# Order of the raw weight loads of a seven-product group: the sum s3 third, the quarter a12 fourth

## The chip, the cores and the metric

The kernel runs on one core of a Trainium2 chip. The metric is the device time of one execution in microseconds. The kernel before takes 1626.28 us, the median of three runs that lie between 1625.93 and 1626.74 us. All times below are microseconds unless ns is written; a time such as "at 1041.06" counts from the first instruction of the profiled execution.

The engines are named as the profile names them: PE does the matrix products (PEld is its weight load, which lies beside them), DVE is the vector engine, ACT the scalar engine, POOL the GpSimd engine, SP the engine that only issues transfers. Each engine works through its own instructions in order.

## The reference

The reference is a decoder trunk of two layers on 512 tokens of width 1024, all in 32-bit floats. Its shape, cut to what matters here:

```python
for l in range(DEPTH):                                   # 2 layers
    x = x + 0.5 * swiglu(rms_norm(x, ...), ffn1_wg[l], ffn1_wu[l], ffn1_wd[l])
    h = rms_norm(x, mix_norm[l])
    z = h @ w_in[l]                                      # attention and short convolution
    x = x + concat([attn_out, conv_out]) @ w_out[l]
    x = x + 0.5 * swiglu(rms_norm(x, ...), ffn2_wg[l], ffn2_wu[l], ffn2_wd[l])
return rms_norm(x, final_norm)

def swiglu(h, w_gate, w_up, w_down):
    return (jax.nn.silu(h @ w_gate) * (h @ w_up)) @ w_down
```

The gate and up weights are 1024 x 2816, the down weights 2816 x 1024, so nearly all the work is the product of 512 tokens with large weight matrices that are each used once. Every weight comes from memory as 32-bit floats.

## The kernel before

**Two words per number.** PE multiplies numbers of a shorter format, so each weight tile is split into two words: ACT casts the raw tile to `wh`, DVE subtracts that from the raw tile and gives the rest, `wl` (both on line 228, function `split`). The activations are split in the same way. A product is then three matrix products: `wh` with the high word, `wh` with the low word, `wl` with the high word.

**Seven products instead of eight.** Most of the weights go through a scheme of the Strassen-Winograd kind. A group takes a matrix of weights as four quarters a11, a12 (first index 0: the gate weights, or the left half of the outputs of a down projection) and a21, a22 (the up weights, or the right half), and multiplies seven forms of them, in this order (`FORMS`, line 38): a11, a12, s2, s3, s1, a22, s4. Signs aside, s1 is a21 with a22 added, s2 is a11 with s1 added, s3 is a21 with a11 added (the gate sum's unit), and s4 is a12 with s2 added. Each form has two halves of 128 x 1024 elements, so a group is 14 half products, and each half product in a feed-forward block is 12 matrix instructions on PE. In the chain of work a whole product (two halves, 24 instructions) is one line.

**Raw units.** The function `seven` (line 375) lists what is loaded for a group, as ten units of 512 KB, two halves each: before the change a11, s1, a12, s3, a22. The units of s1 and s3 have two sources. The first is loaded by SP as all units are (line 210); the second is added on the way by an accumulating transfer that POOL issues (line 223). s2 is made in place of a11 by an addition on DVE (line 269), and s4 in place of a12 (line 291 on DVE; line 289, an accumulating transfer from POOL, in the groups whose `how` is `"share"`).

**What sets the order.** `need_split` (line 236) walks through the list of all forms of the kernel. For each it first calls `need_raw` (line 212), which issues loads up to a given unit, then emits the cast and the subtraction. `take_split` calls it two half products ahead of PE (`SPLIT_AHEAD = 2`). How far the loads run ahead is set by the table `last` and `LOAD_AHEAD = 4`: at form `what`, half `h`, units up to `u + max(last, 4) + h + 4` are asked for, where `u` is the group's first unit. The loads go to SP in the order of the units, whatever the order of their use. They land in a pool of 8 buffers (tag `raw`, line 123), so a load waits until an earlier unit has been used for the last time. The split words have three buffers each (tags `wh` and `wl`, lines 272 and 273): the cast of half product n waits until PE has finished half product n-3.

The order of the instructions on each engine is fixed when the program is built: a scheduler takes them by the order in which they are written and by its own estimate of when each can start. Some orders are forced with `tc.issue_after`. One matters here: in the groups of the down projections, whose s2 is of the kind `"share"`, the DVE addition that makes the first half of s2 comes after the subtraction emitted last, which is that of the second half of a12 (`state["rest"]`, lines 264 to 269).

**Stages.** Each feed-forward block runs a plain stage (`p`), a narrow down projection (`d`), five gate-and-up groups (`w`, at 1, 3, 5, 7, 9), two groups of the down projection (`s`, at 1 and 5) and a last narrow one (`d`); the last block of the kernel ends instead with a group of its own (`e`), whose load and form order stand in `END_LOADS` and `END_FORMS`, apart from those of the other groups. The mixer's `w_out` is one more group. That makes 29 groups that `seven` builds: per layer 10 gate-and-up groups and one of `w_out`, and in all 7 of down projections. In this text the group ("s", 1) of a block is called the *first down group*, ("s", 5) the *second down group*; there are four of the first and three of the second. In a gate-and-up group ACT and DVE also gate the results; in the down groups they add results to the residual, and in the first down group they split the last forms of the activations as well.

Of the kernel before, what the change touches and what calls it, by code (L numbers as in the profile page):

```python
# [75 lines left out]
def trunk_kernel(  # L76
# [118 lines left out]
    raw_of, split_of = {}, {}  # L195
# [4 lines left out]
    def add_unit(*unit):  # L200
        units.append(unit)
        return len(units) - 1
# [24 lines left out]
    def split(hi, lo, raw, eng=nc.vector):  # L227
        return nc.scalar.copy(hi, raw), eng.tensor_sub(lo, raw, f32(hi))  # L228

    def split_far(hi, lo, raw):  # L230

        nc.scalar.activation(lo, raw, AF.Copy, scale=-1.0)
        nc.scalar.copy(hi, raw)
        return nc.gpsimd.dma_start(out=f32(lo), in_=raw, accum_op=ALU.add)

    def need_split(g):
        while state["split"] <= min(g, len(order) - 1):
            n = state["split"]
            u, what = order[n]
            far = what == "far"  # L240
            if what in (None, "far"):
                need_raw(u if far else max(u, min(u + LOAD_AHEAD, state["hold"] or len(units))))
                raw = raw_of.pop(u)
            elif isinstance(what, tuple) and what[0] == "end":

                _, what, h = what
                at = {"a11": 2, "s2": 2, "s3": 3, "s1": 3, "a12": 4, "a22": 5, "s4": 5}[what]
                need_raw(u + 3 * at + h + LOAD_AHEAD)
                raws = {name: u + 3 * i + h for i, name in enumerate(END_LOADS)}
                if what == "s2":  # L250
                    with tc.issue_after(state["rest"]):
                        nc.vector.tensor_add(raw_of[raws["a11"]], raw_of[raws["a11"]], raw_of[raws["s1"]])
                raw = raw_of[raws["a11" if what in ("s2", "s4") else what]]
            elif isinstance(what, tuple):

                what, h, how = what
                far = how == "far"
                last = {"a11": 0, "a12": 4, "s2": 2, "s3": 6, "s1": 2, "a22": 8, "s4": 4}[what]
                need_raw(u + h if far else u + max(last, 4) + h + LOAD_AHEAD)
                a11, s1, a12, s3, a22 = (raw_of.get(u + 2 * i + h) for i in range(5))  # L260
                if what == "s2":

                    late = state["late"] if h else None
                    if not state["late"] and how == "share":
                        late = state["rest"]
                    if how == "behind":
                        late = state["mark"]
                    with tc.issue_after(late) if late else nullcontext():
                        nc.vector.tensor_add(a11, a11, s1)  # L269
                raw = {"a11": a11, "a12": a12, "s2": a11, "s3": s3, "s1": s1, "a22": a22, "s4": a12}[what]  # L270
            shape = list(raw.shape)
            hi = wpool.tile(shape, F32R, tag="wh", bufs=3, name=f"wh_{n}")
            lo = wpool.tile(shape, F32R, tag="wl", bufs=3, name=f"wl_{n}")
            if far:
                sent = split_far(hi, lo, raw)
            else:
                state["cast"], state["rest"] = (i.ins for i in split(hi, lo, raw))
                if isinstance(order[n][1], tuple) and order[n][1][2] == "mark":
                    state["mark"] = state["rest"]
            if isinstance(order[n][1], tuple) and order[n][1][0] == "end":  # L280
                if what == "a12":
                    nc.gpsimd.dma_start(out=raw_of[raws["a11"]], in_=raw, accum_op=ALU.add)
                if what in ("s3", "s1", "a12", "a22"):
                    del raw_of[raws[what]]
                if what == "s4":
                    del raw_of[raws["a11"]]
            elif isinstance(order[n][1], tuple):
                if what == "s3" and how == "share":
                    nc.gpsimd.dma_start(out=a12, in_=a11, accum_op=ALU.add)
                elif what == "s3":  # L290
                    nc.vector.tensor_add(a12, a12, a11)
                done = {"s3": (0, 3), "s1": (1,), "a22": (4,), "s4": (2,)}.get(what, ())
                for i in done:
                    del raw_of[u + 2 * i + h]
            split_of[n] = (hi, lo)
            state["split"] += 1
            if far:

                with tc.issue_after(sent.ins):
                    need_raw(u + LOAD_AHEAD + (4 + h if isinstance(order[n][1], tuple) else 0))  # L300
# [26 lines left out]
    def abreast(kc):  # L327

        return max(1, KC // kc) if kc in (2, 4) else 1
# [34 lines left out]
    def plan():  # L364
        def cols(src, k0, kc, n, how=None, last=False):
            wide = abreast(kc)
            for b in halves_of(n, wide, last):
                order.append((add_unit((src, k0, kc, b * P, wide * P)), how))

        def plain(wg, wu, b):  # L370
            for w in (wg, wu):
                for j in range(2):
                    order.append((add_unit((w, 0, KC, (2 * b + j) * P, P)), None))

        def seven(at, how):


            u = len(units)
            for what in (((0, 0),), ((1, 0), (1, 1)), ((0, 1),), ((1, 0), (0, 0)), ((1, 1),)):
                for h in range(2):  # L380
                    add_unit(*(at(o, j, h) for o, j in what))
            order.extend((u, (what, h, how(what, h))) for what in FORMS for h in range(2))

        def ffn(wg, wu, wd, stages, near=False):
            for what, b in stages:
                how = "far" if b == (0,) and not near else None
                if what == "p":
                    plain(wg, wu, b)
                if what == "w":
                    seven(  # L390
                        lambda o, j, h: ((wg, wu)[o], KC // 2 * j + 2 * h, 2, 2 * b * P, S),
                        lambda what, h: "far"
                        if (b, what, h) == (1, "a11", 0)
                        else {("a12", 0): "mark", ("s2", 1): "behind"}.get((what, h))
                        if near and b == 3
                        else None,
                    )
                if what == "s":
                    seven(
                        lambda o, j, h: (wd, 2 * b + KC // 2 * j + 2 * h, 2, o * S, S),  # L400
                        lambda what, h: None if (b, what) == (1, "s3") else "share",
                    )
                if what == "d":
                    cols(wd, 2 * b[0], 2 * len(b), KC, how, len(b) == 2)
                    if len(b) == 2:
                        closing.append(len(units) - 1)
                if what == "e":
                    u = len(units)
                    roomy.update(range(u, u + 3))
                    for form_ in END_LOADS:  # L410
                        ojs = {"s1": ((1, 0), (1, 1)), "s3": ((1, 0), (0, 0))}
                        for i in range(3):
                            add_unit(
                                *(
                                    (wd, 2 * b + (KC + 2 * j if i == 2 else KC // 2 * j + 2 * i), 2, o * S, S)
                                    for o, j in ojs.get(form_, ((0, int(form_ == "a12")) if form_ != "a22" else (1, 1),))
                                )
                            )
                    order.extend((u, ("end", what, i)) for what in END_FORMS for i in range(3))

        for l in range(DEPTH):
            ffn(ffn1_wg[l], ffn1_wu[l], ffn1_wd[l], INNER, l == 0)
            for c in MIX_COLS:
                for j in range(2):
                    order.append((add_unit((w_in[l], 0, KC, (2 * c + j) * P, P)), None))
            seven(
                lambda o, j, h: (w_out[l], KC // 2 * j + 2 * h, 2, o * S, S),
                lambda what, h: "share",
            )
            ffn(ffn2_wg[l], ffn2_wu[l], ffn2_wd[l], INNER if l + 1 < DEPTH else LAST)  # L430
# [1349 lines left out]
```

## Time and profile before

| What | Value |
|---|---|
| median of three runs | 1626.28 us |
| profiled execution, its own time | 1626.23 us |
| its span, first to last instruction | 1624.4 us |
| PE busy | 1615.6 us, 99% |
| DVE busy | 1376.8 us, 85% |
| ACT busy | 1177.8 us, 73% |
| POOL busy | 216.4 us, 13% |
| granted TensorE clock | 1.000 |
| moved by transfers | 313.92 MB |

The span is the time from the first to the last instruction in the trace; 1.8 us of the profiled execution lie outside it. "Busy" is the time in which an engine has an instruction under way. In the lines of a timeline the columns are the start, the duration, the engine, the source line, the operation, the tiles as output<-inputs, shapes, how many instructions were merged into the line, and in brackets how long the engine was idle before and what ended that. A `q` behind the engine's name means that the engine only issues a transfer. In the list of transfer issues the columns are tiles, issuing engine, operation, count, KB of one, and the median time from issue to landing.

### The profile page before, as it was taken

The page shows a single profiled execution, that of the slowest core. Times are in us where ns is not written, and L with a number is a line of the kernel's source. Part 1 is how long each engine was busy: PE and PEld are TensorE (multiplying, and loading weights), DVE is VectorE, ACT ScalarE, POOL GpSimd, SP SyncE. Part 2 cuts the span into 40 slices and gives each one's busy share as a digit, 9 for nine tenths or more (in the row PEclk, how much of TensorE's full clock was granted, in tenths as well). Part 3 has the DMA queues.
Part 4 walks back from the last instruction along what each step waited for, and adds up shares of the span by engine and source line. Part 5 has one row for each costly group of instructions (what it writes and reads, how often), then busy time and mean ns, then how long its engine had stood idle before and what let it go on. Part 6 is the DMA issues. An engine that isn't in the chain of part 4 may idle for free.

```text
span 1624.4 us, 21158 instructions
## 1 busy us (share of the span) xinstructions
PE 1615.6 (99%) x7571; PEld 1348.7 (83%) x7571; DVE 1376.8 (85%) x1788; ACT 1177.8 (73%) x1511; POOL 216.4 (13%) x191
## 2 busy tenths in 40 slices
PE   9999999999999999999999999999999999999998
PEld 7888888888898888888888888888888988888887
DVE  7978798988899877798998777989688998678997
ACT  6667777857766677778865777788586767878665
POOL 1211111001211111111011111110012111111121
PEclk9999999999999999999999999999999999999999
DMA  9999999823597699999767999998136978999892
GB/s 268 214 232 208 228 208 212 238 60 78 139 228 178 174 224 217 217 211 227 220 143 183 224 214 227 213 220 216 45 91 156 233 149 220 227 220 220 245 228 72
DMA packets 306030, 313.92 MB, mean 193 GB/s; under 512 B 125500, under 2 KB 188548, under 8 KB 305924
## 3 DMA queue, kind: packets, MB, share of 16 engines
q1 hardware_dynamic: 265412, 230.90, 50.0%
q0 software_dynamic: 40048, 81.27, 29.2%
q8 instruction: 59, 0.97, 0.2%
q10 hardware_dynamic: 464, 0.40, 0.1%
q14 instruction: 47, 0.39, 0.1%
HBM read 264.29 MB, written 2.10 MB: 164 GB/s over the span
## 4 chain that ended last, share of the span: by engine, by line
PE 96%; DVE 2%; ACT 1%; DMA 1%; issue 0%; SPq 0%; ACTq 0%; DVEq 0%
PE x L837 27%; PE y L837 13%; PE x_s L837 9%; PE acc L318 7%; PE w L837 7%; PE acc L319 7%; PE acc L321 7%; PE y_s L837 5%; PE x_m L822 3%; PE w_s L837 3%; PE y_m L822 1%; PE y_e L837 1%; PE x_e L837 1%; PE acc L699 1%; PE w_m L822 1%; DVE wl L228 1%
## 5 line engine op out<-in xcount | busy, mean ns | idle before, releaser
L228 DVE TENSOR_TENSOR wl<-raw,wh 128x1024 fp32r<-128x1024 f32 (+1 forms) x494 | 599.1, 1221 | 162.4 <-ACT wh L228 161.0
L228 ACT CAST wh<-raw 128x1024 fp32r<-128x1024 f32 (+1 forms) x494 | 513.7, 1043 | 303.9 <-PE x L837 92.9
L318 PE MATMUL acc<-xh,wh 128*128 128x512 f32 x392 | 153.3, 393 | 0.5 <-ACT wh L228 0.5
L319 PE MATMUL acc<-xl,wh 128*128 128x512 f32 x392 | 153.1, 391 | 0.0
L321 PE MATMUL acc<-xh,wl 128*128 128x512 f32 x384 | 149.6, 390 | 0.0
L223 POOL DMA_DIRECT2D raw<-in_ffn_wu_dram x40 | 50.6, 1277 | 380.6 <-DMA raw<-in_ffn_wu_dram 200.4
L318 PEld LDWEIGHTS acc<-xh,wh 128*128 128x128 f32 x392 | 73.8, 188 | 15.2 <-ACT wh L228 0.6
L319 PEld LDWEIGHTS acc<-xl,wh 128*128 128x128 f32 x392 | 73.7, 188 | 14.4
L321 PEld LDWEIGHTS acc<-xh,wl 128*128 128x128 f32 x384 | 72.1, 188 | 15.2
L223 POOL DMA_DIRECT2D raw<-in_ffn_wd_dram x34 | 41.0, 1218 | 272.9 <-DMA raw<-in_ffn_wd_dram 166.7
L223 POOL DMA_DIRECT2D raw<-in_ffn_wg_dram x40 | 49.0, 1232 | 205.2 <-DMA raw<-in_ffn_wu_dram 105.0
L269 DVE TENSOR_TENSOR raw<-raw,raw 128x1024 f32<-128x1024 f32 x58 | 70.5, 1220 | 3.2 <-DMA raw<-in_ffn_wu_dram 2.0
L1101 ACT COPY raw_a<-turned 128x1024 uint16<-128x1024 uint16 x48 | 63.5, 1357 | 0.0
L837 PE MATMUL x<-wl,ft1h 128*128 128x512 f32 x160 | 62.4, 390 | 0.0
L837 PE MATMUL w<-wh,fb21h 128*128 128x512 f32 x160 | 62.3, 390 | 0.0
L837 PE MATMUL y<-wh,ft3h 128*128 128x512 f32 x160 | 62.3, 390 | 0.0
L837 PE MATMUL x<-wl,ft2h 128*128 128x512 f32 x160 | 62.3, 389 | 0.0
L837 PE MATMUL x<-wh,ft1h 128*128 128x512 f32 x160 | 62.3, 389 | 0.0
L837 PE MATMUL x<-wh,ft2h 128*128 128x512 f32 x160 | 62.3, 389 | 0.0
L837 PE MATMUL x<-wh,ft1l 128*128 128x512 f32 x160 | 62.3, 389 | 0.0
L837 PE MATMUL x<-wh,ft2l 128*128 128x512 f32 x160 | 62.2, 389 | 0.0
L837 PE MATMUL w<-wh,fb21l 128*128 128x512 f32 x160 | 62.2, 389 | 0.0
(517 smaller groups left out, 4546.6 us busy)
## 6 DMA issues: line engine op xcount, KB each, us to landing
raw<-in_ffn_wu_dram SPq DMA_DIRECT2D x127, 512.0 KB, 5.4
raw<-in_ffn_wd_dram SPq DMA_DIRECT2D x105, 512.0 KB, 5.6
raw<-in_ffn_wg_dram SPq DMA_DIRECT2D x86, 512.0 KB, 5.2
raw<-in_ffn_wu_dram POOLq DMA_DIRECT2D x40, 512.0 KB, 9.0
raw<-in_ffn_wg_dram POOLq DMA_DIRECT2D x40, 512.0 KB, 6.2
raw<-in_w_in_dram SPq DMA_DIRECT2D x36, 512.0 KB, 4.0
raw<-in_ffn_wd_dram POOLq DMA_DIRECT2D x34, 512.0 KB, 8.4
raw<-in_w_out_dram SPq DMA_DIRECT2D x20, 512.0 KB, 4.1
```

The source lines that it names most:

```text
L223: nc.gpsimd.dma_start(out=r, in_=rows_of(*more), accum_op=ALU.add)
L228: return nc.scalar.copy(hi, raw), eng.tensor_sub(lo, raw, f32(hi))
L269: nc.vector.tensor_add(a11, a11, s1)
L318: nc.tensor.matmul(acc, hi[:, k, :], rhs[k][0], start=k == first, stop=False)
L319: nc.tensor.matmul(acc, hi[:, k, :], rhs[k][1], start=False, stop=False)
L321: nc.tensor.matmul(acc, lo[:, k, :], rhs[k][0], start=False, stop=k == last)
L699: nc.tensor.matmul(opening[n], (lo if part == "w" else hi)[:, k, :], xl if part == "x" else xh, start=n not in begun, stop=k == KC - 1 and ...
L822: nc.tensor.matmul(accs[c // 2][:, c % 2, :], w[:, k, cols], x_[:, 2 * h + k, :], start=start and c % 2 == 0 and h + k + i == 0, stop=h + ...
L837: nc.tensor.matmul(accs[u], x_[:, 2 * h + k, tok], w[:, k, :], start=start and h + k + i == 0, stop=h + k == 2 and i == 2, skip_group_chec ...
L1101: nc.scalar.copy(words(raws[self.b][:, c, :]), self.to[:, :, c, :])
```

## The change

In `seven` the pairs of units are listed in the order a11, s1, s3, a12, a22 in place of a11, s1, a12, s3, a22. The places of the other units, the order of the seven products and the number and size of the transfers stay as they are. In `need_split` the names are bound to the new places, the entries of `last` follow (a12 and s4 from 4 to 6, s3 from 6 to 4), and so do the places that are dropped after s3 and s4. With the new table the split of a12 asks for units up to `u + 10 + h`, where it asked for `u + 8 + h`; the split of s3 asks for `u + 8 + h`, where it asked for `u + 10 + h`. Units 10 and 11 are the first two of what follows the group.

```diff
-                last = {"a11": 0, "a12": 4, "s2": 2, "s3": 6, "s1": 2, "a22": 8, "s4": 4}[what]
+                last = {"a11": 0, "a12": 6, "s2": 2, "s3": 4, "s1": 2, "a22": 8, "s4": 6}[what]
                 need_raw(u + h if far else u + max(last, 4) + h + LOAD_AHEAD)
-                a11, s1, a12, s3, a22 = (raw_of.get(u + 2 * i + h) for i in range(5))
+                a11, s1, s3, a12, a22 = (raw_of.get(u + 2 * i + h) for i in range(5))
...
-                done = {"s3": (0, 3), "s1": (1,), "a22": (4,), "s4": (2,)}.get(what, ())
+                done = {"s3": (0, 2), "s1": (1,), "a22": (4,), "s4": (3,)}.get(what, ())
...
-            for what in (((0, 0),), ((1, 0), (1, 1)), ((0, 1),), ((1, 0), (0, 0)), ((1, 1),)):
+            for what in (((0, 0),), ((1, 0), (1, 1)), ((1, 0), (0, 0)), ((0, 1),), ((1, 1),)):
                 for h in range(2):
                     add_unit(*(at(o, j, h) for o, j in what))
```

## The prediction

> **What bounds the kernel now.** I read the page's first part, then PE's own waits, then the chain of waits around one first down group (the one at 1038 us), and then that group's transfers, ACT and DVE by their timelines.
>
> ```profile
> span 1624.4 us, 21158 instructions
> PE 1615.6 (99%) x7571; PEld 1348.7 (83%) x7571; DVE 1376.8 (85%) x1788; ACT 1177.8 (73%) x1511; POOL 216.4 (13%) x191
> ...
> PE idle L151 <- DVE warm L646: 1.2, 1, 1.2
> PE acc L318 <- ACT wh L228: 0.5, 1, 0.5
> PE acc L699 <- ACT xh L470: 0.2, 1, 0.2
> ```
>
> PE is the bound: busy 1615.6 of 1624.4 us, and its waits sum to 1.9 us. A change of loads can take next to nothing off; what it can do is make PE wait. Each microsecond for which PE waits is one in the total, since nothing else in the kernel has slack to give back. So the question is where the split words are only just in time.
>
> ```profile
> 1043.97 5.44 PE w_s L837 x24
> 1049.41 5.51 PE x_s L837 x24
> ...
> 1052.42 0.42 PE L837 MATMUL x_s<-wl,ft2h_s 128*128 128x512 f32 x1
> ...
> 1051.07 1.22 DVE L228 TENSOR_TENSOR wl<-raw,wh 128x1024 fp32r<-128x1024 f32 x1
> ```
>
> The first two lines are of the chain of waits: a product takes 5.44 us, but the s2 product of this group 5.51. The other two, of PE's and DVE's timelines, say why: the subtraction for the second half of s2 ends at 1051.07 + 1.22 = 1052.29, and the first instruction that reads this `wl` starts at 1052.42. In a first down group there is no slack at s2. Now DVE and ACT ahead of it:
>
> ```profile
> 1040.53 1.22 DVE L228 TENSOR_TENSOR wl<-raw,wh 128x1024 fp32r<-128x1024 f32 x1
> ...
> 1042.80 1.22 DVE L228 TENSOR_TENSOR wl<-raw,wh 128x1024 fp32r<-128x1024 f32 x1
> 1043.94 1.22 DVE L269 TENSOR_TENSOR raw<-raw,raw 128x1024 f32<-128x1024 f32 x1
> ...
> 1038.34 1.06 ACT L228 CAST wh<-raw 128x1024 fp32r<-128x1024 f32 x1 [0.53 <-PE x L837]
> 1039.30 0.59 ACT L1028 ACTIVATE gate<-x 128x512 f32<-128x512 f32 x1
> 1039.79 1.04 ACT L228 CAST ft4h_s<-sum_s 128x1024 fp32r<-128x1024 f32 x1
> 1041.06 1.06 ACT L228 CAST wh<-raw 128x1024 fp32r<-128x1024 f32 x1 [0.23 <-PE x_s L837]
> ```
>
> The two casts `wh<-raw` are the halves of a12, the two subtractions `wl<-raw` theirs. The addition at 1043.94 makes s2 and is ordered behind the second subtraction. From here to 1052.29 DVE runs nearly one operation behind the other (4.86 of the 5.00 us from 1044 to 1049, in a row below), so what delays a12 here delays s2, and PE with it.
>
> **The change part by part.** No transfer, cast, subtraction or product is added or removed. Two edits count.
>
> *The pairs a12 and s3 change places on SP's queue.* A load waits for a free raw buffer, and buffers come free in the order of the forms, which stays; so I take it that a12 is now issued where s3 was, and lands where s3's first source did, and the other way round.
>
> ```profile
> 1025.40 0.37 SPq L210 DMA_DIRECT2D raw<-in_ffn_wd_dram  x1
> raw<-in_ffn_wd_dram SPq DMA_DIRECT2D x1, 512.0 KB, 5.0
> ...
> 1030.00 0.37 SPq L210 DMA_DIRECT2D raw<-in_ffn_wd_dram  x1
> raw<-in_ffn_wd_dram SPq DMA_DIRECT2D x1, 512.0 KB, 10.8
> ...
> 1033.40 0.37 SPq L210 DMA_DIRECT2D raw<-in_ffn_wd_dram  x1
> raw<-in_ffn_wd_dram SPq DMA_DIRECT2D x1, 512.0 KB, 8.5
> 1041.35 2.44 POOL L223 DMA_DIRECT2D raw<-in_ffn_wd_dram  x2 [12.42 <-DMA raw<-in_ffn_wd_dram]
> ```
>
> These are the first load of a12 in this group, the two of s3's first sources, and the accumulating transfers of s3's second sources, which POOL issues 0.55 us after the first landing. Landings: a12's first half at 1030.4, s3's at 1030.00 + 10.8 = 1040.80 and 1033.40 + 8.5 = 1041.90. The cast of a12's first half stood at 1038.34, so it waits 2.46 us more. The gate and the form t4 stand behind it on ACT, so the second cast moves by 2.46 less the 0.23 us that ACT idled before it, 2.23 us, and with it the second subtraction, the addition, s2 and PE. The second half's landing (1041.90) is then no limit, as its cast comes at 1043.3. Of the other three first down groups I have the issue of s3's first load, its time to landing and the old cast of a12 for two, and POOL's accumulation for the third:
>
> ```profile
> 226.94 0.37 SPq L210 DMA_DIRECT2D raw<-in_ffn_wd_dram  x1
> raw<-in_ffn_wd_dram SPq DMA_DIRECT2D x1, 512.0 KB, 9.1
> 235.28 1.06 ACT L228 CAST wh<-raw 128x1024 fp32r<-128x1024 f32 x1 [0.53 <-PE x L837]
> ...
> 718.50 1.20 POOL L223 DMA_DIRECT2D raw<-in_ffn_wd_dram  x1 [11.41 <-DVE p L1029]
> 715.92 1.06 ACT L228 CAST wh<-raw 128x1024 fp32r<-128x1024 f32 x1 [0.53 <-PE x L837]
> ...
> 1511.62 0.37 SPq L210 DMA_DIRECT2D raw<-in_ffn_wd_dram  x1
> raw<-in_ffn_wd_dram SPq DMA_DIRECT2D x1, 512.0 KB, 10.8
> 1519.97 1.06 ACT L228 CAST wh<-raw 128x1024 fp32r<-128x1024 f32 x1 [0.53 <-PE x L837]
> ```
>
> At 235: 226.94 + 9.1 - 235.28 = 0.76, less 0.23 is 0.5. At 716: the accumulation at 718.50 less the 0.55 seen above gives a landing at 717.95, so 2.03 less 0.23 is 1.8. At 1520: 1511.62 + 10.8 - 1519.97 = 2.45, less 0.23 is 2.2; this group has no residual sums on ACT, so I allow it 0.5 of slack at s2 (an estimate) and take 1.7. Sum of the four: 0.5 + 1.8 + 2.2 + 1.7 = 6.2 us.
>
> *s3's accumulations start earlier and run beside a12's loads.* Before, POOL issued them from 1041.35 on, when the plain loads were through. Now s3's first half lands at 1030.4, 10.4 us sooner, POOL issues its accumulation at once, behind those of s1, and a12's loads share the transfer engines with them.
>
> ```profile
> 1035.00:1037.00 2.00, 2.00 (x10) 1.66 (x9) 2.00 (x4) 1.06 (x1) 0.00 (x0) 1.00 1.09 260
> 1038.00:1039.00 1.00, 1.00 (x6) 0.84 (x5) 1.00 (x3) 0.66 (x1) 0.00 (x0) 1.00 1.06 387
> 1044.00:1049.00 5.00, 5.00 (x23) 4.13 (x23) 4.86 (x6) 4.38 (x6) 0.00 (x0) 1.00 1.08 195
> ```
>
> The last column of these stretches is GB/s with the engines fully busy (the share before it): 387 with plain loads alone, 195 with accumulations alone, 260 with both. An accumulation of 512 KB (524 kB) thus takes 2.7 us of all transfer engines, a load 1.35. If one accumulation gets between, a12's second half lands up to 2.7 us later than the 1041.90 above, at 1044.6, and its cast is 1.3 us behind the 1043.3 already counted; if none does, 0. For four groups 0 to 5.2 us; I take the middle, 2.6, because the stretch with both shows them sharing, while the accumulations of s1 stand ahead of s3's in the queue. The Trainium skill ("DMA: Bandwidth & Descriptors", section "Queues, rings and completion order") says that each transfer engine takes turns between the queue rows that have work. By that rule the loads would keep half of the engines' turns until s3's accumulations are through, which speaks against the change and puts this term at its upper end, 5.2 us; the trace agrees as far as 260 lies between 195 and 387.
>
> *The other groups.* In a gate-and-up group the cast of a12 waits for PE rather than for its load:
>
> ```profile
> 915.56 0.37 SPq L210 DMA_DIRECT2D raw<-in_ffn_wu_dram  x1
> raw<-in_ffn_wu_dram SPq DMA_DIRECT2D x1, 512.0 KB, 6.6
> 925.73 1.07 ACT L228 CAST wh<-raw 128x1024 fp32r<-128x1024 f32 x1
> ...
> 1071.60 0.37 SPq L210 DMA_DIRECT2D raw<-in_ffn_wd_dram  x1
> raw<-in_ffn_wd_dram SPq DMA_DIRECT2D x1, 512.0 KB, 8.0
> 1079.22 1.06 ACT L228 CAST wh<-raw 128x1024 fp32r<-128x1024 f32 x1 [0.41 <-PE x_s L837]
> ```
>
> Here a12 would land at 915.56 + 6.6 = 922.2, 3.6 us ahead of its cast at 925.73: cost 0, hidden by the wait for a `wh` buffer. In the second down group the last half lands at 1079.6 against a cast at 1079.22: 0.4 late, 3.1 with one accumulation between. For the three of them 0 to some 6 us; I take 0, the end that the row is nearest to, and leave the rest to the range. The groups next to a narrow projection I did not price one by one; I allow them 0 to 3 us.
>
> *The further look-ahead.* The split of a12 now asks for two more units than before and that of s3 for two fewer. The loads stand in the same order on SP, each behind a buffer that comes free no sooner; SP's transposes between them may change places. I price it at 0. If the cover (SP's idle time between bursts) is gone, a transpose or a load is late by one product, 5.44 us.
>
> The sum: 1626.23 + 6.2 + 2.6 = 1635.0 us, against the profiled execution (span 1624.4 and 1.8 outside it), which stands 0.05 below the median 1626.28.
>
> **The rivals.**
>
> *Hidden.* The instruction order is made anew for the changed kernel. If gate and t4 come ahead of the a12 cast on ACT, the cast at 1040.80 costs little: second cast at 1041.9, first subtraction at 1041.9, the second at 1043.1, against 1042.80 now. Four groups at 0.2 to 0.3 us give 1626.23 + 1 = 1627 us, not slower by what can be told. For it: the scheduler orders by when it thinks data arrive. Against it: it has to know of the crowded queues, and the addition behind the second subtraction is forced in any case. It decides where a12 is cast no later than 0.3 us after its place now.
>
> *Worse.* The extra units asked for at a12 put loads ahead of transposes, or in the last block take buffers from operands (its first three units come from the activations' pool). One product's delay, 5.44 us, at three places on top of the sum gives 1635.0 + 16.3 = 1651 us. Nothing in the profile of before speaks for it but the single SP queue.
>
> *Faster.* s3's sums are complete earlier. That helps only where PE waits for s3, and the rows of PE's waits show no such place; even all 1.9 us of them would give 1624.3, which is within 0.2%.
>
> **How the numbers follow.** 0.2%, 3.25 us, is about what a measurement of this kernel can tell from no change. The forecast, PE held up at s2 in the down groups, 1629.5 to 1646: 0.73. Hidden: 0.16, 1626 to 1629. Worse: 0.09. Faster: 0.02. Slower by over 0.2% is 0.73 + 0.09 = 0.82; within 0.2%, 0.16. The predicted time is that of the forecast, 1635. The range runs from 1627 (half of the hidden case is below it) to 1646, which is 1626.2 + 6.2 + 5.2 + 6 + 3 rounded down; it leaves out 0.08 + 0.09 + 0.02 = 0.19. The forecast's own range is 1629.5 to 1646.
>
> **What would show it.** In the profile after, the chain of waits has s2 products of 6 to 9 us in the four first down groups instead of 5.5, and PE's waits name `wl` or `wh` of line 228 there; ACT idles before the cast of a12 until a load lands; POOL issues s3's accumulations 5 us or more sooner; the gate-and-up groups keep 5.44 us per product. I am wrong if a12's cast stays where it is (hidden), if s2 is on time although a12 is late (DVE's order has changed), or if the lost time lies in gate-and-up groups, at transposes or in the last block.

## The result, and the profile after

The changed kernel takes 1652.42 us, the median of six runs (1650.74 to 1655.8), against 1626.51 for the kernel before on the same chip: a ratio of 1.016, with a 95% interval of 1.0149 to 1.0171. It is 26 us slower. The direction was foreseen; the size was not: the forecast was 1635.0, and 1652 lies above the range of 1627 to 1646.

The first part of the profile page after, with the engines' share of the chain of waits, and then PE's own waits (total in us, how often, the longest):

```profile
span 1649.9 us, 21154 instructions
PE 1626.5 (99%) x7571; PEld 1348.6 (82%) x7571; DVE 1379.6 (84%) x1788; ACT 1173.3 (71%) x1511; POOL 215.7 (13%) x191
...
PE 81%; DVE 8%; DMA 5%; ACT 3%; issue 2%; SPq 0%; ACTq 0%; DVEq 0%
```

```profile
PE x_s L837 <- DVE wl L228: 7.3, 9, 1.5
PE w_s L837 <- ACT wh L228: 3.8, 1, 3.8
PE x_m L822 <- DVE ft2l_m L228: 1.7, 2, 0.9
PE idle L151 <- DVE warm L646: 1.2, 1, 1.2
PE y_s L837 <- DVE wl L228: 0.9, 2, 0.5
```

Before, PE waited for 1.9 us in all, and never for a split weight of a seven-product group. Now it waits for `wl` and `wh` of line 228 in the down groups (`_s`) and for a form of the activations in `w_out` (`_m`). These waits add up to less than the 25.5 us by which the span grew, because the matmuls next to a wait run slower too: around the wait of 1.51 us shown below, 1.68 us are lost from start to start and 0.11 more on the next matmul. In one place the clock comes on top. So I measure PE's lost time in another way: for each two successive matmuls, the time from start to start less the usual one of that shape (227 ns for 128x512), summed over a stretch. For the whole kernel this gives 5.3 us before and 30.7 after. The 25.4 us between are the whole loss, and 23.3 of them lie here:

| Stretch | before | after | without s3's accumulations (below) | the same, s2 free |
|---|---|---|---|---|
| down groups, layer 1, first block (from 235) | 0.0 | 3.2 | 1.3 | -0.1 |
| down groups, layer 1, second block (from 721) | 0.0 | 6.0 | 2.2 | 0.5 |
| down groups, layer 2, first block (from 1049) | 0.0 | 4.0 | 1.6 | 0.5 |
| down group of the last block (from 1537) | 0.0 | 8.1 | 2.1 | 0.0 |
| the two groups of `w_out` | 0.2 | 2.2 | 0.2 | 0.4 |

(Times of the profile after; the loss of a stretch differs by up to 3 us between profiled executions of kernels that agree there: 4.0 in the third row, 7.2 with the new order in the down groups alone.)

In the first down group at 1049 the mechanism is the one forecast. These are pieces of the chain of waits through it (start, duration, what), and the two instructions on PE's timeline at which s2 stalls:

```profile
1044.46 10.99 DMA raw<-in_ffn_wd_dram
...
1055.54 1.06 ACT wh L228
...
1056.62 1.23 DVE wl L228
1057.85 1.15 DVE raw L269
...
1060.16 1.22 DVE wl L228
...
1064.73 3.47 DVE wl L228 x3
```

```profile
1061.44 0.50 PE L837 MATMUL x_s<-wl,ft2h_s 128*128 128x512 f32 x1 [0.46 <-DVE wl L228]
...
1065.98 0.50 PE L837 MATMUL x_s<-wl,ft2h_s 128*128 128x512 f32 x1 [1.51 <-DVE wl L228]
```

The load of a12's second half is issued at 1044.46 and is under way for 10.99 us; 0.1 us after it lands the cast starts, then the subtraction, then the addition of line 269 that had to wait for it, and behind it the two halves of s2's `wl`, at 1060.16 and 1064.73. PE waits for both, and 0.6 and 1.7 us are lost from start to start. The group starts 11.06 us later than before (the cast of its first a11 half went from 1032.90 to 1043.96). In that frame a12's first cast moved by 2.1 us (from 1038.34 to 1051.52) and its second by 3.4 (from 1041.06 to 1055.54), against 2.46 forecast and 2.2 to 3.5. POOL's issues of s3's accumulations in this group:

```profile
1041.22 1.19 POOL L223 DMA_DIRECT2D raw<-in_ffn_wd_dram  x1 [1.88 <-DVE wl L228]
1048.00 1.20 POOL L223 DMA_DIRECT2D raw<-in_ffn_wd_dram  x1 [5.58 <-DVE wl L228]
```

The last block is another matter. First the chain of waits, then the ACT timeline, then a table of stretches (PE busy, PEld, DVE, ACT, POOL, the granted PE clock, the share of the transfer engines, GB/s):

```profile
1532.44 16.14 DMA raw<-in_ffn_wd_dram
...
1548.68 1.05 ACT wh L228
```

```profile
1541.35 1.04 ACT L228 CAST ft4h_s<-sum_s 128x1024 fp32r<-128x1024 f32 x1
1548.68 1.04 ACT L228 CAST wh<-raw 128x1024 fp32r<-128x1024 f32 x1 [6.29 <-DMA raw<-in_ffn_wd_dram]
```

```profile
1549.70:1552.60 2.90, 2.79 (x6) 1.79 (x7) 2.84 (x3) 0.02 (x1) 0.00 (x0) 0.50 0.00 0
1552.60:1555.40 2.80, 2.80 (x8) 2.12 (x7) 2.80 (x4) 1.05 (x1) 0.00 (x0) 0.51 0.00 0
1555.40:1556.00 0.60, 0.60 (x7) 0.58 (x6) 0.60 (x2) 0.00 (x0) 0.00 (x0) 1.00 0.00 0
```

Here a12's second half was under way for 16.14 us, PE stood still for 3.8, and its clock was granted at half speed from 1548.5, still within the stall, to 1555.3. The twelve matmuls from 1549.78 on took 5.6 us where 2.7 are usual, 2.9 us on top of the stall. Why the load was so long under way shows in the order of SP's loads in this block, taken from the two programs, before (-) and after (+). In the new kernel 13404 and 13407 are the halves of s3, 13410 and 13412 those of a12, and 13462 and 13480 the first two units of the closing group; in the old one 13404 and 13406 are a12, 13408 and 13411 s3:

```
 L210 DMACopy raw_13404<-in_ffn_wd_dram 128x2x512
-L210 DMACopy raw_13406<-in_ffn_wd_dram 128x2x512
-L210 DMACopy raw_13408<-in_ffn_wd_dram 128x2x512
-L210 DMACopy raw_13411<-in_ffn_wd_dram 128x2x512
+L210 DMACopy raw_13407<-in_ffn_wd_dram 128x2x512
+L210 DMACopy raw_13410<-in_ffn_wd_dram 128x2x512
+L210 DMACopy raw_13462<-in_ffn_wd_dram 128x2x512
+L210 DMACopy raw_13480<-in_ffn_wd_dram 128x2x512
+L210 DMACopy raw_13412<-in_ffn_wd_dram 128x2x512
```

The closing group's first units have buffers of their own, in the activations' pool (`roomy`). They are now asked for at a12's split, need not wait for a raw buffer, and so go out ahead of a12's second half.

### The profile page after: what moved, and what is told of

It reads as the page before. It is cut to its first block, busy times and chain, and to the rows that moved or that the text cites. A ratio compares the mean times of both kernels' runs of the same rounds, so it can differ in the third digit from the quotient of the medians.

```text
span 1649.9 us, 21154 instructions
## 1 busy us (share of the span) xinstructions
PE 1626.5 (99%) x7571; PEld 1348.6 (82%) x7571; DVE 1379.6 (84%) x1788; ACT 1173.3 (71%) x1511; POOL 215.7 (13%) x191
## 4 chain that ended last, share of the span: by engine, by line
PE 81%; DVE 8%; DMA 5%; ACT 3%; issue 2%; SPq 0%; ACTq 0%; DVEq 0%
PE x L837 23%; PE y L837 12%; PE acc L318 7%; PE acc L319 7%; PE acc L321 7%; PE w L837 6%; PE x_s L837 4%; DMA raw<-in_ffn_wd_dram 4%; DVE wl L228 3%; PE y_s L837 3%; PE x_m L822 3%; PE y_m L822 1%; ACT wh L228 1%; PE w_s L837 1%; PE y_e L837 1%
## 5 line engine op out<-in xcount | busy, mean ns | idle before, releaser
L837 PE MATMUL w<-wl,fb21h 128*128 128x512 f32 x160 | 62.4, 390 | 0.0
```

The lines of the kernel that those rows point to most:

```text
L837: nc.tensor.matmul(accs[u], x_[:, 2 * h + k, tok], w[:, k, :], start=start and h + k + i == 0, stop=h + k == 2 and i == 2, skip_group_chec ...
```

## The experiments

The theory after the two traces: a12 now lands only just in time everywhere; in the down groups and `w_out`, where there is no slack behind it, that becomes a wait of PE. It lands late for two reasons, its later place on SP's queue and s3's accumulations, which share the transfer engines with it; the new look-ahead adds to this in the last block alone. Rivals: the loss is spread over all 29 groups; the place alone makes it; the look-ahead costs everywhere or nowhere.

**Where: one kind of group at a time.** In three kernels the new order and table hold for one kind of group, the old ones for the rest:

```diff
-            for what in (((0, 0),), ((1, 0), (1, 1)), ((1, 0), (0, 0)), ((0, 1),), ((1, 1),)):
+            mid = [((1, 0), (0, 0)), ((0, 1),)] if new else [((0, 1),), ((1, 0), (0, 0))]
+            for what in (((0, 0),), ((1, 0), (1, 1)), *mid, ((1, 1),)):
```

> The new load order and table in the twenty gate-and-up groups alone; the down groups and w_out keep the old. Theory A (the loss sits where a12 was already cast within a few us of its landing: the down groups and w_out): 1626 to 1628 us, no change, and no PE wait at s2. Rival B (the loss is spread over all 29 groups, since each group's a12 lands some 10 us later): 20/29 of 26 us, 1644 us.

Measured: 1629.72 us against 1626.34, a ratio of 1.002 (1.0011 to 1.003).

> The new order and table in the seven groups of the down projections alone. Theory A: PE's lost time in the down groups of the changed kernel, read segment by segment, is 3.2 + 6.0 + 4.0 + 8.1 = 21.3 us, so 1647 to 1650 us. Rival B: 7/29 of 26 us, 1633 us.

Measured: 1648.38 us, 1.013 (1.0113 to 1.0147).

> The new order and table in the two groups of w_out alone. Theory A: two stalls of 1.0 us each at the x_m product and little besides, 1628 to 1630 us. Rival B: 2/29 of 26 us, 1628 us. If the stalls of w_out came from a shift handed on by the down groups before them, 1626.5 us.

Measured: 1628.46 us, 1.0014 (1.0004 to 1.0023), with the same two waits `x_m <- ft2l_m` as in the changed kernel, so they are `w_out`'s own. (Theory A and rival B had named about the same time here, so this run does not tell them apart.)

The down groups carry 22.0 us, `w_out` 2.1, the twenty gate-and-up groups 3.4; the sum, 27.5, is the 26 of the whole within its interval. Rival B falls. But the gate-and-up groups were expected at nothing. Of ACT's waits, these are the ones for a load, before, then after:

```profile
ACT wh L228 <- DMA raw<-in_ffn_wg_dram: 0.7, 1, 0.7
```

```profile
ACT wh L228 <- DMA raw<-in_ffn_wg_dram: 39.3, 25, 2.9
...
ACT wh L228 <- DMA raw<-in_ffn_wd_dram: 22.1, 10, 6.3
...
ACT wh L228 <- DMA raw<-in_w_out_dram: 11.1, 2, 6.1
```

`in_ffn_wg` is where a11 and a12 of a gate-and-up group come from. ACT now waits for such a load 25 times; the cast has slack enough there that PE hardly sees it, but the slack is used up.

**The look-ahead.** The changed kernel with the old table, and the kernel before with the new one:

```diff
-                last = {"a11": 0, "a12": 6, "s2": 2, "s3": 4, "s1": 2, "a22": 8, "s4": 6}[what]
+                last = {"a11": 0, "a12": 4, "s2": 2, "s3": 6, "s1": 2, "a22": 8, "s4": 4}[what]
```

> The changed kernel with the old look-ahead table (a12 and s4 at 4, s3 at 6), so that the new load order stands alone. Theory A: the table costs only in the last block, where the loads of the closing group's first two units pass a12's second half on SP; without that the stall of 4.0 us at w_s there, and the 2.9 us of slow matmuls behind it, fall to the 2 to 3 us of the other first down groups: 1646 to 1648 us. Rival C (the look-ahead changes nothing, the stall in the last block is the late place and the shared transfer engines, as elsewhere): 1652 us.

Measured: 1648.65 us, 1.0141 (1.0125 to 1.0156): 3.8 less than the changed kernel, just above what theory A had named. The interval overlaps that of the changed kernel (1.0149 to 1.0171), so the times alone leave the size open; the traces are clearer. SP's order in the last block is a12, a12, without the closing group's units between; no wait of 3.8 us and no halved clock is left there, and PE loses 2.6 us in that block where it lost 8.1. In the third row of the table above this execution lost 6.8 where the changed kernel lost 4.0, so the time fell by less than the block.

> The kernel before with the new look-ahead table alone (a12 and s4 at 6, s3 at 4; old load order). In the last block the loads of the closing group's first two units now pass the second half of s3 on SP. Theory A (the passing costs where the load that is passed is needed next): s3 is needed two products after a12 and has slack, so 1626.5 to 1630 us, and nothing outside the last block. Rival E (the look-ahead by itself takes buffers or turns from every group): 1632 us or more.

Measured: 1626.43 us, 0.9999 (0.999 to 1.0009). In this kernel the same two loads pass s3's second half, and it costs nothing. So the look-ahead costs only through what it passes: a load that is needed next.

**Place or sharing.** The changed kernel without the accumulating transfers of s3's second sources, in the down groups and `w_out`:

```diff
-                    add_unit(*(at(o, j, h) for o, j in what))
+                    add_unit(*(at(o, j, h) for o, j in (what[:1] if bare and what == ((1, 0), (0, 0)) else what)))
```

> The changed kernel without the accumulating transfers of s3's second sources in the down groups and w_out (the sum s3 is left incomplete there, so the output is not the reference's; the plain loads keep their places). Theory A1 (half of the loss is a12 sharing the transfer engines with these accumulations): a12's second half lands 1.5 to 4 us sooner, the s2 stalls of the groups at 235, 721 and 1049 fall from 2.3-2.9 to 0.5-2.2 us, the second down groups and w_out lose theirs (3.1 and 2.2 us): 1641 to 1645 us. Theory A2 (the later place on SP's queue alone): landings and time as in the changed kernel, 1652 us.

Measured: 1635.62 us, 1.0058 (1.0043 to 1.0073). It gives back 16.8 us, more than theory A1 had named. By the table above, 8.1 of them lie in the down groups of the first three blocks, 6.0 in the last block, where the look-ahead has a part in it, and 2.0 in `w_out`. SP's timeline and list of transfer issues for a12's second half in the group that stands at 1042 here, and PE's waits:

```profile
1037.34 0.37 SPq L210 DMA_DIRECT2D raw<-in_ffn_wd_dram  x1
```

```profile
raw<-in_ffn_wd_dram SPq DMA_DIRECT2D x1, 512.0 KB, 7.7
```

```profile
PE x_s L839 <- DVE wl L228: 4.9, 4, 1.5
```

The load takes 7.7 us from issue to landing where it took 10.99, in the same place of the queue; the accumulations of s1 are still under way beside it. What is left among the waits is one at s2 in each of the four first down groups, 4.9 us together and 5.6 from start to start.

> The kernel before, with the accumulating transfers of s3's second sources left out in the down groups and w_out, as in the changed kernel without them (s3 is incomplete there, so the output is not the reference's). If the 17 us that their absence gave the changed kernel are the price of sharing with a12's loads, nothing is to be gained where a12 has landed before they start: 1625.5 to 1626.5 us. If they cost by themselves (engine turns, POOL's queue): well below 1626, down to 1610 us.

Measured: 1626.45 us, 1.0000 (0.9991 to 1.001). In the old order, where a12 has landed before they start, the same transfers cost nothing; with the later landing above, the 16.8 us are the price of their running beside a12's loads.

> The new order in the gate-and-up groups alone, and there without the accumulating transfers of s3's second sources (s3 is incomplete in these groups, so the output is not the reference's). With the new order alone these groups cost 3.4 us (1629.7), and in the changed kernel most of their a12 casts stand 0.1 us behind the landing. Theory A1 (the shared transfer engines take the slack, and now and then more): 1626 to 1627.5 us, and a12 lands some 3 us ahead of its cast. Theory A2 (the later place by itself): 1629 to 1631 us.

Measured: 1627.22 us, 1.0003 (0.9994 to 1.0013), in place of 1629.72. Its wait for these loads:

```profile
ACT wh L228 <- DMA raw<-in_ffn_wg_dram: 7.7, 4, 4.2
```

In these groups alone, with the accumulations, it was 32.3 us in 18 waits. The cast of a12's second half now stands 2.0 us behind the landing (the middle one of 18 groups); it was 0.1 with the accumulations and 6.6 in the kernel before (the middle one of 16). So the later place takes the larger part of the slack, and the sharing takes what is left of it.

**Holding the accumulations back.** POOL issues s3's accumulations only after a12's subtraction of the same half:

```diff
+                if isinstance(order[n][1], tuple) and what == "a12" and u + 4 + h in waits:
+                    seen = nc.gpsimd.tensor_copy(tick, f32(lo)[:, 0, 0:1])
+                    with tc.issue_after(seen.ins):
+                        nc.gpsimd.dma_start(out=s3, in_=rows_of(*units[u + 4 + h][1]), accum_op=ALU.add)
```

> The changed kernel, with POOL holding back the accumulating transfers of s3's second sources in the down groups and w_out until a12's subtraction of the same half is done (a POOL copy of one column of that wl stands ahead of each). Theory A1 (sharing): a12's second half lands 1.5 to 4 us sooner than in the changed kernel and the s2 stalls shrink as without these transfers; s3's sum is then complete some 10 us after a12's subtraction, about when its cast is due, so 0 to 3 us per group come back as waits at y_s: 1641 to 1655 us. Theory A2: the s2 stalls stay, and waits at y_s come on top, 1652 to 1665 us.

Measured: 1653.08 us, 1.0165 (1.0147 to 1.0183): nothing won, and a time that both theories allow. But the loss has moved. In the down groups PE loses 11.4 us (3.8, 2.8, 3.1 and 1.8) in place of 21.3, and in `w_out` 11.2 in place of 2.2. PE's waits:

```profile
PE x_s L846 <- DVE wl L229: 5.9, 4, 1.5
PE y_m L831 <- DMA ft4l_m<-sums_m: 3.0, 1, 3.0
PE x_m L831 <- DMA ft1l_m<-m: 2.6, 2, 2.1
```

In `w_out` POOL also issues the transfers that make the activations' low words (`ft4l_m`, `ft1l_m`), and they now stand in POOL's queue behind the held ones: `ft1l_m` takes 11.6 and 12.0 us from issue to landing in the two groups, where it took 6.7 and 7.7 in the changed kernel.

> The new order in the down groups alone (1648.4 by itself), with POOL holding back s3's accumulating transfers there until a12's subtraction of the same half. In the changed kernel with them held in w_out too, PE lost 3.8 + 2.8 + 3.1 + 1.8 = 11.4 us in the down groups. Theory A1 (sharing is more than half of the loss in these groups): 1626.4 + 11.4, 1636 to 1640 us. If the hold only moves the loss to y_s: 1645 us or more.

Measured: 1639.90 us, 1.0086 (1.0069 to 1.0102), 8.5 below the new order in the down groups without the hold. It lies within what theory A1 had named, and is still 13 us behind the kernel before.

**The order on DVE.** The addition that makes s2 is no longer forced behind a12's second subtraction, in the changed kernel and in the one without s3's accumulations:

```diff
                     if not state["late"] and how == "share":
-                        late = state["rest"]
+                        late = None
```

> The changed kernel without the forced order on DVE: the addition that makes s2 needn't come after the subtraction emitted last, that of a12's second half, and the scheduler now puts it ahead of that. Theory A (a late a12 reaches PE through this order, at s2): the stalls at s2, 0.6 and 1.7 us in each of the groups at 235, 721 and 1049, go, and up to 1 us of stall at a12's own second half stands in their place; the 4 us at w_s in the last block stay: 1644 to 1648 us. Rival D (a12 late is a wait of PE in any case, only shown elsewhere): 1652 us.

Measured: 1649.30 us, 1.0139 (1.0124 to 1.0154), just outside what was expected. PE's waits:

```profile
PE w_s L837 <- ACT wh L228: 3.6, 2, 3.4
PE w_s L837 <- DVE wl L228: 3.0, 4, 1.6
PE x_m L822 <- DVE ft2l_m L228: 1.7, 2, 0.9
...
PE x_s L837 <- DVE wl L228: 1.1, 3, 0.4
```

The waits at s2 (`x_s`) fall from 7.3 to 1.1 us, but in the last block and the second down groups PE now waits at a12's own product (`w_s`). The time fell by 3.1 us against the changed kernel, where the two waits at s2 alone had cost 6.9 in three of the blocks; with a12 as late as this, rival D is right for more than half.

> The changed kernel without s3's accumulating transfers in the down groups and w_out (1635.6 by itself; s3 is incomplete there, so the output is not the reference's), and also without the forced order that puts the s2 addition behind a12's second subtraction. What the later place alone costs is then left to a12's own wait. If the place reaches PE through the forced order: the stalls of 1.2 to 1.6 us at s2 in the four first down groups (5.6 us together) go, 1629 to 1631 us. If it reaches PE anyway: 1635 us.

Measured: 1630.22 us, 1.0027 (1.0017 to 1.0038), 5.4 below the kernel without the accumulations alone. No wait of a down group is left among PE's waits. So the later place by itself reached PE through the forced order and, but for about 1 us (the 0.5 and 0.5 of the table), only through it. The rest, 3.9 us, is about the 3.4 of the gate-and-up groups, which were left as in the changed kernel.

## Why the prediction was right or wrong

**The bound, and the place of the loss: right.** PE had nothing to give back and lost what it was made to wait, but for the last block, where the clock made a stall of 3.8 us cost 2.9 more; the first down groups stall at s2, a12's cast waits for its load, and POOL issues s3's accumulations sooner (11.2 and 5.5 us in the group's frame: 1041.22 and 1048.00 less 11.06, against 1041.35 and 1042.48).

**The first term, a12 in s3's place: right.** It was 6.2 us. With the sharing taken away the four first down groups stall at s2 by 1.3, 1.2, 1.5 and 1.6, together 5.6, and freeing the forced order gives 5.4 back. The single forecasts were 0.5, 1.8, 2.2 and 1.7, off by up to 0.8 us either way, so it is partly luck that the sum came nearer than its parts.

**The second term, s3's accumulations beside a12's loads: the step that failed.** It was taken at 2.6 with 5.2 as its upper end; measured, it is 16.8 in the down groups and `w_out`, and some 2.5 in the gate-and-up groups. In the group that was worked out it was no bad estimate: 2.2 for the place and 0.65 for the sharing were foreseen; 2.3 us were lost at s2, 1.5 of them without the sharing. It failed in what it was applied to. It was charged to the four first down groups, one accumulation each, on top of a delay that was already there. But in the profile after a12's second half lands 0.1 us ahead of its cast in every down group:

- The first down groups at 235, 721 and 1049 lost 2.3 us each at s2; 6.45 had been forecast for the three.
- The other 6.3 us in these blocks lie elsewhere, 4.6 of them in the second down groups. There the prediction took 0 and kept 6 in the range, with the sum already written down: 0.4 us late, 3.1 with one accumulation between. It took the end nearest to the row without the sharing.
- `w_out` lost 2.2 us and was not priced. In one of its two groups, ACT waited 6.1 us for a12's load with the activations' forms queued behind it.
- The last block lost 8.1 us against 2.35.

**Round robin.** The rule cited from the Trainium skill ("DMA: Bandwidth & Descriptors", section "Queues, rings and completion order"), that a transfer engine takes turns between the queue rows with work, pointed to the upper end, and the runs agree with its direction: 10.99 us from issue to landing with s3's accumulations pending, 7.7 without. In the frame of the group worked out, a12's second half landed at 1044.4, close to the 1044.6 of the upper end, and without these accumulations at 1041.1, somewhat ahead of the 1041.90 counted. So the delay in one group was well sized; the number of places that it reached was not. In three microseconds of the profile after, from 1047 to 1050, the two rows of queues read (packets, MB, share of the 16 engines' time):

```profile
q0 software_dynamic: 203, 0.38, 68.9%
q1 hardware_dynamic: 207, 0.40, 40.6%
```

The accumulations (q0) and the loads (q1) moved nearly the same number of packets and bytes, as equal turns would have it, but the accumulations held 1.7 times as much of the engines' time. Equal turns are not equal time when one side's packets take longer. (The 387 GB/s that the prediction read as plain loads alone belong to a stretch with 12 packets of accumulations beside 190 of loads, which changes little.)

**The gate-and-up groups: 0 taken, 3.4 measured.** The 3.6 us of slack was read from one half of one group, and it had not been set against the sharing. Worked out in the same way from the profile before, a12's second half has between -0.4 and 6.2 us in 18 of these groups, 1.8 in the middle one, and in 15 of them less than the 2.7 us of one accumulation. The group that was read is one of the widest. In the profile after, the cast of the second half stands 0.1 us behind its landing in 17 of 18 groups. Where exactly PE loses it isn't shown: in the profiled execution of the new order in these groups alone PE lost 7.8 us in all, 2.5 more than before, and about 0.7 us of that in the first 9 us of the kernel, at loads of `x`. Leaving the accumulations out takes 2.5 of the 3.4 away.

**The look-ahead: 0 taken, 3.8 measured.** The text said that the loads stand in the same order on SP, each behind a buffer. That holds for all units but the roomy ones, and the rival *Worse* had named these. By the prediction's own sign of being wrong, lost time in the last block, it was: 8.1 of the 25.4 us lie there. *Worse* had the place, gave it 0.09, and had the wrong price (a product at three places) and the wrong resource (buffers, and transposes that are passed); in fact two loads pass a12's second half, at one place. There the parts come together: a stall of 3.8 us, and the halved clock behind it. Held accumulations (1.8 us lost there), left-out ones (2.1) or the old table (2.6) each remove most of it.

The sum by runs: 5.4 (place, through the forced order), 16.8 (sharing in the down groups and `w_out`, the last block's look-ahead within it) and 3.4 (gate-and-up groups) make 25.6 of the 26 us. The range failed because its upper end, 1646, added the upper ends of the priced terms and held nothing for the look-ahead and the clock in the last block, for `w_out` or for the gate-and-up groups.

## What to carry to other kernels

A load order is more than an order of landings: moving a unit with a second, accumulating source forward also moves that second transfer, here by 5 to 11 us, into the time of the loads behind it. Price such sharing at each group whose margin between landing and first use is below the delay, and take those margins from all groups and both halves, not from one. And look for requests that wait for no buffer: when they are asked for earlier, they pass whatever does wait.

## What the runs showed of the hardware

PE stood still for 3.82 us in the last block of the changed kernel. Its granted clock fell from 1.00 to 0.50 at 1548.52, 2.6 us after the last matmul had ended, and came back at 1555.34, 6.83 us later; the twelve matmuls in that time cost 2.9 us beside the stall. With s2's order freed, a stall of 3.38 us at the same place was followed by 3.41 us at 0.50. But the length of a wait does not decide alone. In `w_out` of the kernel that holds the accumulations back, a wait of 3.00 us in one group left the clock at 1.00, and one of 2.11 us in the other was followed by 3.41 us at 0.50. These are the matmuls that waited, each with the stretch behind it (PE busy, PEld, DVE, ACT, POOL, the granted PE clock):

```profile
491.60 0.39 PE L831 MATMUL y_m<-ft4l_m,wh 128*128 128x256 f32 x1 [3.00 <-DMA ft4l_m<-sums_m]
491.60:495.00 3.40, 3.40 (x28) 3.40 (x29) 2.70 (x6) 2.17 (x5) 0.00 (x0) 1.00 1.12 322
...
1298.73 0.39 PE L831 MATMUL x_m<-ft1l_m,wh 128*128 128x256 f32 x1 [2.11 <-DMA ft1l_m<-m]
1299.10:1302.40 3.30, 3.30 (x18) 3.30 (x17) 3.30 (x7) 0.58 (x2) 0.00 (x0) 0.50 1.07 243
```

Waits of 1.5 us in the down groups left it at 1.00. The Trainium skill ("TensorE: Matmul & The Clock Gate", section "Part 1: The HAM clock gate") says that the clock halves after at least one idle window of about 3.4 us. The trace does not bear this out as a length of idle time: 2.11 us were enough once, and 3.00 us were not. For the return the Trainium skill gives at least one busy window of about the same length in the same section; the spells of 3.41 and 6.83 us, one and two such lengths, agree with that. What decided between the two waits no run here shows.
